# Projections with stationary weights: four high products, then four low ones

## The chip, the cores and the metric

The kernel runs on one core of one Trainium2 chip. The metric is the device time of one execution in microseconds (us); for the kernel before it is the median of three runs, 1385.38 us.

## The reference

One layer of a hybrid block on a sequence of 256 tokens with 2048 features, all in fp32. The input is normalised and multiplied with one wide matrix; its columns feed 16 attention heads of 128 (three dilated windows over the same keys), a chunked state-space scan (64 heads of 64, 8 groups, state 128) behind a short convolution, and several gates. Cut to what matters here:

```python
hn = rms_norm(x, norm_w)
proj = hn @ w_in                       # (256, 2048) @ (2048, 22592)
q, k, v, z_a, z_s, xbc, dt_raw, g_a, g_s = jnp.split(proj, split_points, axis=-1)
# attention: three (window, dilation) patterns over q, k, v, joined by their log-sum-exp
o_a = o_a.reshape(b, s, ATTN_WIDTH) * jax.nn.silu(z_a)
xbc = jax.nn.silu(causal_depthwise_conv(xbc, conv_w, conv_b))
xs, bm, cm = jnp.split(xbc, ...)
y = ssd_chunked_scan(xs, dt, a, bm, cm) + d_skip * xs
y = rms_norm(y * jax.nn.silu(z_s), ssm_norm_w)
merged = jax.nn.sigmoid(g_a) * (o_a @ w_attn_branch) + jax.nn.sigmoid(g_s) * (y @ w_ssm_branch)
return rms_norm(x + merged @ w_out, final_norm_w)
```

## The kernel before

**Split products.** Each fp32 operand of a large product is cut into a high part in the faster fp32r type and a low part, the rest. A product of two such operands is the sum of high x high, high x low and low x high. The input stands transposed in `XT`: for each of 16 blocks of 128 features (`KT`, index `kt`) 512 columns, 256 tokens of the high part followed by 256 tokens of the low part.

**Weights.** They come in units of 128 x 1024 in the order of a plan. `unit` (lines 269 to 281) waits for one unit `w`, has ScalarE write its high part `h` (L276) and VectorE its low part `l` (L277), and lets later work hang on that unit. Five buffers hold loaded units, four each hold `h` and `l`; a scheduler that orders instructions by priority and a modelled time line lays the streams of all engines, and units are split ahead at raised priority.

**Two ways to use them.** For wide outputs (`gemm_b`, `gemm_pair`: the gates, the value projection, the output matrices) a block of the input is the stationary operand and the weights stream through as 512 columns. For outputs that are needed transposed (B, C, xs, zs, q, k, za) `gemm_a` does the reverse: 128 x 128 weights are stationary and the input streams. A projection is 2 units of 8 blocks, and for each block two products go to one accumulator of 512 columns:

- high, L329: `h` is loaded as the stationary operand, all 512 columns of `XT` stream (high x high in the left half, high x low in the right),
- low, L332: `l` is loaded, the left 256 columns of `XT` stream, and their products are added to the right half.

`evac` adds both halves. There are 124 such projections: B and C for seven groups, 31 xs and 31 zs, 16 each of q, k and za.

**Other places named below.** `gemm_first` (L377 high, L378 low) computes four projections at once at the start, four accumulators for each block of the input; `gemm_dt` (L354) puts high and low weights into one stationary block; `gates` calls `gemm_b` (L412 to L414). Small jobs of the scan and of attention (transposes, scores, masks) are queued with a due time; `tick` and `run_due` in `gemm_a` release them at a projection's start and behind its first product.

Of the kernel before, what the change touches and what calls it, by code (L numbers as in the profile page):

```python
# [16 lines left out]
S = 256  # L17
# [6 lines left out]
KT = D // P  # L24
UNIT = 1024
UK = 8
UB = 2
SCALE = float(P) ** -0.5
L_AHEAD = 120
M_AHEAD = 200  # L30
# [166 lines left out]
def hybrid_block(ctx: ExitStack, tc: tile.TileContext, wall, xt, x, pk_d, cst_d, fw_d, out):  # L197
    nc = tc.nc
    ve, ac, gp, pe = nc.vector, nc.scalar, nc.gpsimd, nc.tensor
# [24 lines left out]
    def bank(tag, bufs, name):  # L224
        return ps.tile([P, 512], F32, name=name, tag=tag, bufs=bufs)
# [41 lines left out]
    def unit(n, shape):  # L267
        if n not in loaded:
            load(n)
        w = loaded.pop(n)  # L270
        h = stream.tile([P, UNIT], F32R, name=f"h{n}", tag="h", bufs=H_BUFS)
        l = stream.tile([P, UNIT], F32R, name=f"l{n}", tag="l", bufs=H_BUFS)
        cuts = (0, UNIT // 2, UNIT) if n < N_FINE else (0, UNIT)
        with tc.high_priority(L_AHEAD) if n >= KT // UB else nullcontext():
            for a, b in zip(cuts, cuts[1:]):
                ac.activation(h[:, a:b], w[:, a:b], AF.Copy)  # L276
                ve.tensor_tensor(l[:, a:b], w[:, a:b], h[:, a:b].bitcast(F32), ALU.subtract)  # L277
        for f in on_unit.pop(n, ()):
            f(h[:, 0:1].bitcast(F32))
        k, m = shape  # L280
        return h.rearrange("p (k m) -> p k m", k=k), l.rearrange("p (k m) -> p k m", k=k)
# [18 lines left out]
    now = [0]  # L300
# [6 lines left out]
    def run_due(until):  # L307
        while True:
            ready = [d for d in due if d[0] <= until]
            if not ready:  # L310
                break
            d = min(ready, key=lambda e: e[0])
            due.remove(d)
            d[1]()

    def tick(final=False):
        now[0] += 1
        run_due(float("inf") if final else now[0])

    def gemm_a(tag, xs_of, acc=None):  # L320
        tick()
        name = f"{tag[0]}{tag[1]}"
        acc = bank(acc, 2, f"ps_{name}") if acc else bank("g", 4, f"ps_{name}")
        for u in range(KT // UK):
            h, l = unit(FIRST[tag] + u, (UK, P))
            for kk in range(UK):
                kt = u * UK + kk
                m = xs_of(kt)
                pe.matmul(acc, h[:, kk, :], m, start=(kt == 0), stop=False)  # L329
                if kt == 0:  # L330
                    run_due(now[0] + 0.5)
                pe.matmul(acc[:, S:], l[:, kk, :], m[:, :S], start=False, stop=(kt == KT - 1))  # L332
        return acc

    def gemm_dt(src):
# [23 lines left out]
    def project(tag, acc=None):  # L359
        return gemm_a(tag, lambda kt: XT[:, kt, :], acc)  # L360

    def gemm_first(tag, prepare, load_on):
        name = f"{tag[0]}{tag[1]}"
        accs = [bank("g", 4, f"ps_{name}_{j}") for j in range(4)]
        for u in range(KT // UB):
            if u % 2 == 0:
                tick()
            for kk in range(UB):
                prepare(u * UB + kk)
            h, l = unit(FIRST[tag] + u, (UB, 512))  # L370
            load_on(u)
            for kk in range(UB):
                kt = u * UB + kk
# [273 lines left out]
    def load_on(u):  # L647
        if u:
            load(u + 4)
        if u < 3:  # L650
            nc.sync.dma_start(xr[:, 2 * u + 10 : 2 * u + 12, :], xt[:, 2 * u + 10 : 2 * u + 12, :])
        if u == 3:
            nc.sync.dma_start(pk[:, KT:], pk_d[:, KT:])
# [31 lines left out]
    with tc.tile_pool(name="ssm", bufs=2) as sp:  # L685
# [223 lines left out]
        for g in range(GROUPS):  # L909
# [9 lines left out]
            for t in range(max(4 * g, 1), 4 * g + 4):  # L919
                u, i = divmod(t, 2)  # L920
                acc = project(("xs", t))
# [19 lines left out]
                acc = project(("zs", t))  # L941
# [91 lines left out]
    with tc.tile_pool(name="att", bufs=2) as ap:  # L1033
# [4 lines left out]
        def scores(h, q, k, p):  # L1038
# [4 lines left out]
            slope = 2.0 ** (-8.0 * (h + 1) / NH)  # L1043
            ve.scalar_tensor_tensor(t, dist_c, slope / SCALE, sps[:, :384], ALU.mult, ALU.add)
            st = ap.tile([P, 8], F32, name=f"st{h}", tag="st", bufs=1)
            parts = ((0, P), (P, 384))
            for i, (a, b) in enumerate(parts):
                ve.tensor_reduce(st[:, i : i + 1], t[:, a:b], mybir.AxisListType.X, ALU.max)
            ve.tensor_scalar(st[:, 2:4], st[:, 0:2], -SCALE, None, ALU.mult)
            for i, (a, b) in enumerate(parts):  # L1050
                ac.activation(p[:, a:b], t[:, a:b], AF.Exp, scale=SCALE, bias=st[:, 2 + i : 3 + i])
            for i, (a, b) in enumerate(parts):
# [219 lines left out]
```

## Time and profile before

| | before |
|---|---|
| three runs | 1384.97, 1385.54, 1385.38 us |
| median | 1385.38 us |
| span of the profiled execution, first to last instruction | 1383.8 us |
| mean granted TensorE clock | 0.998 |
| products on TensorE (PE) | 7266 |
| splits into high and low parts, L276 and L277 | 398 instructions each |
| HBM traffic | 314.87 MB read, 28.77 MB written |

The profiled execution's own time outside its span was not recorded; the median stands 1.6 us above the span. In the profile, PE is TensorE's products and PEld its loads of stationary operands, which overlap them; DVE is VectorE, ACT ScalarE, POOL GpSimd, SP the queue that issues most transfers. A row of the timeline gives the start in us, the duration in us, the engine, the source line, the operation, the tile written and the tiles read, the shapes, and how many equal instructions were merged into the row. Since products are pipelined, the duration of one reaches past the start of the next.

### The profile page before, as it was taken

How to read it: one execution, taken by the hardware profiler on the slowest of the kernel's cores; microseconds unless marked ns; L12 is line 12 of the kernel's file. 1: busy time of each engine (PE TensorE's matmuls, PEld its weight loads, DVE VectorE, ACT ScalarE, POOL GpSimd, SP SyncE). 2: the span in 40 equal slices, each digit the busy share in tenths (PEclk: the TensorE clock that was granted, in tenths of full speed). 3: DMA queues.
4: the chain of work that ended last, by engine and by line, in shares of the span. 5: the costliest groups of instructions: out<-in, count | busy, mean ns of one | idle time of the engine just before them, and what ended most of it. 6: DMA issues, size and time to landing. Idle time of an engine off the chain costs nothing.

```text
span 1383.8 us, 20696 instructions
## 1 busy us (share of the span) xinstructions
PE 1373.6 (99%) x7266; PEld 1169.9 (85%) x7266; DVE 1169.5 (85%) x1753; ACT 835.5 (60%) x1306; POOL 142.0 (10%) x226
## 2 busy tenths in 40 slices
PE   9999999999999999999999999999999999999997
PEld 8888888888888888888888888888888888888886
DVE  7898999987799898789889897777877788888897
ACT  7656677675667675766565554544544556655564
POOL 2301111101011100010001001111111000000112
PEclk9999999999999999999999999999999999999999
DMA  9767988868787866668677668888888757865773
GB/s 347 231 187 225 313 254 291 279 224 287 245 266 240 294 212 208 188 224 280 230 259 267 222 209 278 275 275 273 299 288 301 241 161 264 294 222 180 243 273 122
DMA packets 105080, 345.00 MB, mean 249 GB/s; under 512 B 11728, under 2 KB 13712, under 8 KB 104976
## 3 DMA queue, kind: packets, MB, share of 16 engines
q1 hardware_dynamic: 103536, 339.62, 74.0%
q10 hardware_dynamic: 1440, 4.06, 0.8%
q8 instruction: 57, 0.93, 0.3%
q14 instruction: 47, 0.39, 0.1%
HBM read 314.87 MB, written 28.77 MB: 248 GB/s over the span
## 4 chain that ended last, share of the span: by engine, by line
PE 97%; DMA 1%; DVE 1%; ACT 1%; issue 0%; SPq 0%; POOL 0%; POOLq 0%; DVEq 0%; ACTq 0%
PE ps_zs L329 8%; PE ps_xs L329 8%; PE ps_zs L332 4%; PE ps_q L329 4%; PE ps_za L329 4%; PE ps_k L329 4%; PE ps_xs L332 4%; PE ps_ssm L476 3%; PE ps_ssm L477 3%; PE ps_ssm L478 3%; PE ps_q L332 2%; PE ps_k L332 2%; PE ps_za L332 2%; PE ps_gs L414 2%; PE ps_gs L412 2%; PE ps_gs L413 2%
## 5 line engine op out<-in xcount | busy, mean ns | idle before, releaser
L276 ACT ACTIVATE h<-w 128x1024 fp32r<-128x1024 f32 (+1 forms) x398 | 413.9, 1047 | 318.0 <-issue 78.8
L277 DVE TENSOR_TENSOR l<-w,h 128x1024 fp32r<-128x1024 f32 (+1 forms) x398 | 479.4, 1211 | 124.2 <-ACT h L276 121.8
L329 PE MATMUL ps_zs<-XT,h 128*128 128x512 f32 x496 | 176.3, 397 | 0.0
L329 PE MATMUL ps_xs<-XT,h 128*128 128x512 f32 x496 | 175.9, 396 | 0.0
L332 PE MATMUL ps_zs<-XT,l 128*128 128x256 f32 x496 | 139.9, 282 | 0.0
L332 PE MATMUL ps_xs<-XT,l 128*128 128x256 f32 x496 | 139.8, 282 | 0.0
L329 PEld LDWEIGHTS ps_xs<-XT,h 128*128 128x128 f32 x496 | 93.3, 188 | 21.7
L329 PEld LDWEIGHTS ps_zs<-XT,h 128*128 128x128 f32 x496 | 93.4, 188 | 21.2
L332 PEld LDWEIGHTS ps_zs<-XT,l 128*128 128x128 f32 x496 | 93.7, 189 | 1.5 <-issue 0.7
L332 PEld LDWEIGHTS ps_xs<-XT,l 128*128 128x128 f32 x496 | 93.7, 189 | 0.4
L329 PE MATMUL ps_q<-XT,h 128*128 128x512 f32 x256 | 92.5, 405 | 0.2 <-ACT h L276 0.2
L329 PE MATMUL ps_k<-XT,h 128*128 128x512 f32 x256 | 89.9, 395 | 0.0
L329 PE MATMUL ps_za<-XT,h 128*128 128x512 f32 x256 | 89.7, 394 | 0.0
L543 ACT ACTIVATE ha<-wa 128x1024 fp32r<-128x1024 f32 x43 | 45.4, 1055 | 46.4 <-DMA wa<-in_wall 10.9
L332 PE MATMUL ps_q<-XT,l 128*128 128x256 f32 x256 | 71.2, 278 | 0.0
L332 PE MATMUL ps_k<-XT,l 128*128 128x256 f32 x256 | 71.1, 278 | 0.0
L332 PE MATMUL ps_za<-XT,l 128*128 128x256 f32 x256 | 71.1, 278 | 0.0
L544 DVE TENSOR_TENSOR la<-wa,ha 128x1024 fp32r<-128x1024 f32 x43 | 52.5, 1220 | 11.9 <-ACT ha L543 11.8
L782 ACT ACTIVATE gt<-acb,acT 128x128 f32<-128x128 f32 x128 | 44.2, 391 | 23.7 <-DMA acb<-acum_d 21.9
L329 PEld LDWEIGHTS ps_q<-XT,h 128*128 128x128 f32 x256 | 48.2, 188 | 11.5 <-ACT h L276 0.6
L329 PEld LDWEIGHTS ps_za<-XT,h 128*128 128x128 f32 x256 | 48.1, 188 | 11.3
L329 PEld LDWEIGHTS ps_k<-XT,h 128*128 128x128 f32 x256 | 48.1, 188 | 11.2
(688 smaller groups left out, 3325.1 us busy)
## 6 DMA issues: line engine op xcount, KB each, us to landing
w<-in_wall SPq DMA_DIRECT2D x394, 512.0 KB, 4.7
wa<-in_wall SPq DMA_DIRECT2D x43, 512.0 KB, 4.9
th_a<-in_wall SPq DMA_DIRECT2D x19, 512.0 KB, 5.6
sums_at<-in_wall SPq DMA_DIRECT2D x18, 512.0 KB, 4.7
acb<-acum_d SPq DMA_DIRECT2D x32, 256.0 KB, 4.0
t_ssm<-sums_at SPq DMA_DIRECT2D x13, 512.0 KB, 4.1
wt<-t_ssm SPq DMA_DIRECT2D x13, 512.0 KB, 5.4
th_a<-in_wall SPq DMA_DIRECT2D x19, 256.0 KB, 6.0
```

The lines of the kernel that those rows point to most:

```text
L276: ac.activation(h[:, a:b], w[:, a:b], AF.Copy)
L277: ve.tensor_tensor(l[:, a:b], w[:, a:b], h[:, a:b].bitcast(F32), ALU.subtract)
L329: pe.matmul(acc, h[:, kk, :], m, start=(kt == 0), stop=False)
L332: pe.matmul(acc[:, S:], l[:, kk, :], m[:, :S], start=False, stop=(kt == KT - 1))
L412: pe.matmul(accs[i], xh, h[:, kk], start=(kt == 0), stop=False)
L413: pe.matmul(accs[i], xh, l[:, kk], start=False, stop=False)
L476: pe.matmul(acc, xh, h, start=start, stop=False)
L477: pe.matmul(acc, xh, l, start=False, stop=False)
L478: pe.matmul(acc, xl, h, start=False, stop=stop)
L543: ac.activation(h, src, AF.Copy)
L544: ve.tensor_tensor(l, src, h.bitcast(F32), ALU.subtract)
L782: ac.activation(g4[:, n, b], acb[:, j, b // 2 * P : b // 2 * P + P], AF.Relu, scale=-1.0, bias=sc[:, h : h + 1],)
```

## The change

In `gemm_a` the eight blocks of a unit are taken in two runs of four (`A_RUN = 4`). Within a run the four high products come first and the four low ones after them. Before, each high product was followed by the low product of its block. The operands, shapes, accumulators and the flags that start and end an accumulation are those of before; the due jobs are still released behind the first product of a projection.

```diff
+A_RUN = 4
...
         for u in range(KT // UK):
             h, l = unit(FIRST[tag] + u, (UK, P))
-            for kk in range(UK):
-                kt = u * UK + kk
-                m = xs_of(kt)
-                pe.matmul(acc, h[:, kk, :], m, start=(kt == 0), stop=False)
-                if kt == 0:
-                    run_due(now[0] + 0.5)
-                pe.matmul(acc[:, S:], l[:, kk, :], m[:, :S], start=False, stop=(kt == KT - 1))
+            for k0 in range(0, UK, A_RUN):
+                for kk in range(k0, k0 + A_RUN):
+                    kt = u * UK + kk
+                    pe.matmul(acc, h[:, kk, :], xs_of(kt), start=(kt == 0), stop=False)
+                    if kt == 0:
+                        run_due(now[0] + 0.5)
+                for kk in range(k0, k0 + A_RUN):
+                    kt = u * UK + kk
+                    pe.matmul(acc[:, S:], l[:, kk, :], xs_of(kt)[:, :S], start=False, stop=(kt == KT - 1))
```

The lines below it move by three, `gemm_a`'s own to L330 (high) and L335 (low). What becomes of it on PE, first at the end of a projection of xs (the tiles `h` and `l` are the parts of one unit, numbers tell buffers apart), where the next one, zs, begins. Before:

```order
L332 MATMUL ps_xs_4292<-XT,l_4296 128x256
L329 MATMUL ps_xs_4292<-XT,h_4295 128x512
L332 MATMUL ps_xs_4292<-XT,l_4296 128x256
L329 MATMUL ps_xs_4292<-XT,h_4317 128x512
L329 MATMUL ps_zs_4356<-XT,h_4359 128x512
L332 MATMUL ps_xs_4292<-XT,l_4318 128x256
L329 MATMUL ps_xs_4292<-XT,h_4317 128x512
L332 MATMUL ps_xs_4292<-XT,l_4318 128x256
L329 MATMUL ps_xs_4292<-XT,h_4317 128x512
```

After:

```order
L330 MATMUL ps_xs_4292<-XT,h_4317 128x512 x4
L335 MATMUL ps_xs_4292<-XT,l_4318 128x256 x4
L330 MATMUL ps_xs_4292<-XT,h_4317 128x512 x4
L335 MATMUL ps_xs_4292<-XT,l_4318 128x256 x4
L330 MATMUL ps_zs_4356<-XT,h_4359 128x512 x4
L335 MATMUL ps_zs_4356<-XT,l_4360 128x256 x4
```

High and low products took turns before, but for one product of zs that the scheduler had drawn ahead, so that two high ones stood together; now they stand in fours, and here zs begins behind xs.

The second place is a projection of B with small jobs inside it (`dt_tp` transposes, `cbp` scores of the scan). Before:

```order
L329 MATMUL ps_B_1195<-XT,h_1198 128x512
L742 MATMUL dt_tp<-cst,early 128x64 x2
L768 MATMUL cbp_1024<-ct_401,bt_400 128x256
L769 MATMUL cbp_1024<-ct_401,bt_400 128x128
L742 MATMUL dt_tp<-cst,early 128x64 x2
L332 MATMUL ps_B_1195<-XT,l_1199 128x256
```

After:

```order
L335 MATMUL ps_B_1195<-XT,l_1199 128x256 x2
L745 MATMUL dt_tp<-cst,early 128x64 x2
L771 MATMUL cbp_1024<-ct_401,bt_400 128x256
L772 MATMUL cbp_1024<-ct_401,bt_400 128x128
L335 MATMUL ps_B_1195<-XT,l_1199 128x256 x2
L330 MATMUL ps_B_1195<-XT,h_1198 128x512 x4
L335 MATMUL ps_B_1195<-XT,l_1199 128x256 x2
L745 MATMUL dt_tp<-cst,early 128x64 x2
L335 MATMUL ps_B_1195<-XT,l_1199 128x256 x2
```

The jobs stood in one group between a high and a low product; now they stand in two groups, each inside a run of low ones.

## The prediction

> **What bounds the kernel now.** I read the busy table first, then the chain that ended last, then what TensorE waited for. On the page:
>
> ```profile
> PE 1373.6 (99%) x7266; PEld 1169.9 (85%) x7266; DVE 1169.5 (85%) x1753; ACT 835.5 (60%) x1306; POOL 142.0 (10%) x226
> PEclk9999999999999999999999999999999999999999
> PE 97%; DMA 1%; DVE 1%; ACT 1%; issue 0%; SPq 0%; POOL 0%; POOLq 0%; DVEq 0%; ACTq 0%
> ```
>
> In the table of waits on PE:
>
> ```profile
> PE warm L623 <- DVE ssq L620: 1.4, 1, 1.4
> PE ps_first L377 <- ACT h L276: 0.3, 1, 0.3
> PE ps_q L329 <- ACT h L276: 0.2, 1, 0.2
> ```
>
> TensorE is busy 99% of the span, is 97% of the last chain, has its full clock in every slice, and waits for other engines 1.9 us in all, 1.4 us of them before the first product. So the time is the number of products times the spacing at which TensorE starts them. A product's listed duration overlaps the next product, so spacings have to be read from starts. How many products the change touches, by stage (line 329 alone; the x behind PE busy is the count):
>
> ```profile
> 74.00:558.00 484.00, 427.01 (x1216) 228.28 (x1216) 1.00 0.78 252
> 828.00:1120.00 292.00, 270.13 (x767) 144.21 (x767) 1.00 0.82 273
> ```
>
> By the code there are 124 projections of 16 pairs: 1984 pairs, each one high product (512 columns, L329) and one low (256 columns, L332). The two windows hold 1983 of the high ones.
>
> **What one pair costs now.** The timeline of PE in two stretches where only these pairs run. From 533.20 to 549.10 there are 45 of each, from 317.92 to 346.00 there are 81 (first and last row of each):
>
> ```profile
> 533.20 0.40 PE L329 MATMUL ps_xs<-XT,h 128*128 128x512 f32 x1
> ...
> 549.10 0.40 PE L329 MATMUL ps_xs<-XT,h 128*128 128x512 f32 x1
> ```
>
> ```profile
> 317.92 0.39 PE L329 MATMUL ps_B<-XT,h 128*128 128x512 f32 x1
> ...
> 346.00 0.39 PE L329 MATMUL ps_zs<-XT,h 128*128 128x512 f32 x1
> ```
>
> 15.90 us / 45 = 353.3 ns, and 28.08 us / 81 = 346.7 ns. The same instructions in the same order run at two spacings, each held for tens of us. All the steps from one high product to the next over one low one, from the first to the last below, are 1908 in the timeline and average 349.4 ns: about four tenths of them long.
>
> ```profile
> 76.79 0.39 PE L329 MATMUL ps_xs<-XT,h 128*128 128x512 f32 x1
> ...
> 1119.20 0.39 PE L329 MATMUL ps_za<-XT,h 128*128 128x512 f32 x1
> ```
>
> What turns the short spacing into the long one can be seen where one projection overlaps the next and two high products stand together:
>
> ```profile
> 387.40 0.39 PE L329 MATMUL ps_C<-XT,h 128*128 128x512 f32 x1
> ...
> 390.87 0.39 PE L329 MATMUL ps_xs<-XT,h 128*128 128x512 f32 x1
> 391.10 0.39 PE L329 MATMUL ps_zs<-XT,h 128*128 128x512 f32 x1
> ...
> 391.44 0.40 PE L329 MATMUL ps_xs<-XT,h 128*128 128x512 f32 x1
> ...
> 392.85 0.40 PE L329 MATMUL ps_xs<-XT,h 128*128 128x512 f32 x1
> ```
>
> Ten pairs up to 390.87 take 3.47 us (347 ns each); after the double the four pairs from 391.44 take 1.41 us (352 ns each). So the strict turn high, low, high, low can hold the short spacing, and breaking the turn can lose it.
>
> **The change, part by part.** It removes nothing and adds nothing: the same 1984 + 1984 products, loads of stationary weights, transfers, splits and evictions. It moves three low products of every four behind the high ones. On PE 475 runs of exactly four high and 488 of four low come out, so it does what it says; the few other products (transposes, scores, scan) stand in 58 groups where there were 57. No wait is added. A low half is first needed three high products later than before, a high half of a unit is read out one run of low ones earlier; with the waits above near zero neither gain is worth anything, and the cover is that both halves are ready ahead now. If it were gone, the price is what such a wait costs, 0.2 to 0.3 us each by those rows. On SP, POOL, ACT and DVE some neighbours swap places; no transfer waits show on PE, so I take zero.
>
> What is left is the spacing in runs of four. The kernel has a place that already does this: the first projection (L377 high, L378 low, four accumulators) starts its units in runs of four and four, its later ones partly in turn. PE timeline there:
>
> ```profile
> 10.87 1.08 PE L377 MATMUL ps_first<-yTa,h 128*128 128x512 f32 x4
> 12.25 1.09 PE L377 MATMUL ps_first<-yTa,h 128*128 128x512 f32 x4
> 13.18 0.63 PE L378 MATMUL ps_first<-yTa,l 128*128 128x256 f32 x4
> 13.65 1.09 PE L377 MATMUL ps_first<-yTa,h 128*128 128x512 f32 x4
> ...
> 19.27 0.40 PE L377 MATMUL ps_first<-yTb,h 128*128 128x512 f32 x1
> ...
> 20.66 1.09 PE L377 MATMUL ps_first<-yTb,h 128*128 128x512 f32 x4
> ...
> 22.06 0.40 PE L377 MATMUL ps_first<-yTb,h 128*128 128x512 f32 x1
> ...
> 23.47 1.11 PE L377 MATMUL ps_first<-yTb,h 128*128 128x512 f32 x4
> ...
> 24.89 0.40 PE L377 MATMUL ps_first<-yTb,h 128*128 128x512 f32 x1
> ...
> 26.28 1.08 PE L377 MATMUL ps_first<-yTb,h 128*128 128x512 f32 x4
> ...
> 27.67 0.40 PE L377 MATMUL ps_first<-yTb,h 128*128 128x512 f32 x1
> ```
>
> Nine blocks of four and four: 10.87 to 12.25 (1.38 us), five in a row from 12.25 to 19.27 (7.02), then 1.40, 1.42 and 1.39. Together 12.61 us / 36 pairs = 350.3 ns; the five in a row alone 351.0; the cheapest 345 to 347, the dearest 355. Within a block (12.25, 13.18, 13.65) the high four take 0.93 us (232 ns each) and the low four 0.47 us (117.5 ns each). So runs neither reach the short spacing for good nor fall to something new.
>
> A run of products of one shape alone, for comparison: the gate stage (L412 to L414, all 512 columns, 40 products between the first two rows), and the dt projection, 16 high-width products in a row that start out of step:
>
> ```profile
> 60.93 0.39 PE L414 MATMUL ps_gs<-h,yTa 128*128 128x512 f32 x1
> ...
> 69.99 0.39 PE L412 MATMUL ps_gs<-h,yTb 128*128 128x512 f32 x1
> ```
>
> ```profile
> 29.08 2.03 PE L354 MATMUL ps_dt<-yTa,h 128*128 128x512 f32 x8
> 30.94 1.98 PE L354 MATMUL ps_dt<-yTb,l 128*128 128x512 f32 x8
> 32.77 0.39 PE L412 MATMUL ps_gs<-h,yTa 128*128 128x512 f32 x1
> ```
>
> 9.06 / 40 = 226.5 ns steady; in the dt projection the first eight take 232.5 ns each and the next eight 229: settling takes more than eight products, a run of four is too short for it. A short pair (346.7) is 226.5 plus 120 for the low product.
>
> The sum: (350.3 - 349.4) ns x 1984 = +1.8 us. Bounds from the rows: all pairs at the short spacing, -2.7 x 1984 = -5.4 us; all at the long one, +3.9 x 1984 = +7.7 us; all as the dearest block, +5.6 x 1984 = +11 us. I take the mean of the nine blocks, the nearest rows there are. The profiled span is 1383.8 us, the median 1385.4 us, so 1.6 us lie around it; span 1385.6 us, time **1387.2 us**.
>
> A rule that speaks against any effect: the Trainium skill, SBUF — State Buffer, section Who interferes with whom, gives TensorE two independent read ports, one for the moving operand and one for weight loads. By it the place of the loads would not change the spacing, and the sum would be 0. The two spacings above, for one and the same order, are not explained by that rule, but no row shows that the loads cause them.
>
> **The rivals.**
>
> *The short spacing holds in runs* (25%). For it: the blocks from 10.87 and from 26.28 took 345 and 347 ns per pair, and in the attention stage the turn holds the short spacing almost throughout, so a good start after each head could last. Against: in the first projection it was lost again within one block. Price -2 to -5.4 us, 1380.0 to 1383.4 us.
>
> *Runs hold the long spacing: the slower side* (23%). Each change from four high to four low breaks the turn as the double at 391.10 did, and four products are too few to settle. It decides from 350.8 ns per pair on (1.4 ns x 1984 = 2.8 us). At 351.0, the five blocks in a row, 1388.6 us; at 353.3, 1393.1 us. Against: the mean over nine blocks lies below.
>
> *Low runs get cheaper than any row* (6%). Were a low run to cost half of a steady 512-column product, 113 ns, the pair would be 226.5 + 113 = 339.8 ns, -9.6 x 1984 = -19 us, 1366 us. Against it: the low four at 117.5 ns above. The skill has such a rule: TensorE: Matmul & The Clock Gate, section Back-to-back issue gap, gives columns / 2.4 + 2.5 ns for an isolated spacing, 216 and 109 ns; a pair of 325 would be an estimate of -48 us. The steady 226.5 ns disagrees with it, and the measurement decides.
>
> *The weight load shows* (1%). A load lasts 189 ns:
>
> ```profile
> L332 PEld LDWEIGHTS ps_zs<-XT,l 128*128 128x128 f32 x496 | 93.7, 189 | 1.5 <-issue 0.7
> ```
>
> If loads could not overlap, a low run would go at 189 ns and the pair at 416: +130 us. The four low at 117.5 ns exclude it, since loads then overlap.
>
> **How the numbers follow.** The forecast itself, a mixture of both spacings between 349 and 350.8 ns, -1 to +2.8 us, has 45%. A measurement of this kernel tells 0.2% (2.8 us) from no change. Faster by more: most of the short-spacing rival and the cheap low runs, 22 + 6 = 28%. Slower by more: the long-spacing rival, the load and a little of the forecast's upper end, 28%. Within: 44%. Range 1380 to 1392 us: from all pairs short to most pairs long; outside lie the cheap low runs and the dearest blocks. The forecast's own range is 1384.4 to 1388.2 us.
>
> **What would show it.** In the new profile, starts from one run of four high to the next, divided by four: near 350 ns with blocks of both kinds proves the step; 346.7 throughout the attention stage proves the first rival; 351 to 353 throughout the second; low runs at 113 the third. Waits on PE beyond 3 us, or more groups of other products among the runs, would make the step that takes the rest as zero wrong.

## The result and the profile after

| | before | after |
|---|---|---|
| median of 20 runs each on one chip | 1385.51 us (1384.77 to 1386.75) | 1388.12 us (1387.19 to 1389.09) |
| ratio after / before, 95% interval | | 1.0019 (1.0013 to 1.0025) |
| span of the profiled execution | 1383.8 us | 1386.5 us |
| mean granted TensorE clock | 0.998 | 0.999 |

The change costs 2.6 us, at the edge of the 0.2% that were called no change. The forecast was 1387.2 us.

From the page of the changed kernel, the busy table and the chain that ended last by engine:

```profile
PE 1376.0 (99%) x7266; PEld 1172.5 (85%) x7266; DVE 1170.0 (84%) x1753; ACT 837.6 (60%) x1306; POOL 145.9 (11%) x226
PE 97%; DMA 1%; DVE 1%; ACT 1%; issue 0%; SPq 0%; POOL 0%; POOLq 0%; DVEq 0%; ACTq 0%
```

The table of waits on PE has two rows left:

```profile
PE warm L626 <- DVE ssq L623: 1.4, 1, 1.4
PE ps_first L380 <- ACT h L277: 0.6, 1, 0.6
```

The same number of products, the same bound, 2.0 us of waits where there were 1.9. The 2.4 us that PE is busy for longer are spacing. The stages show where. These are the first products of the value projection, of the gate stage behind attention, and of the attention branch's output in the timeline of before (the first product of xs, 76.79, stands in the prediction):

```profile
748.54 0.39 PE L476 MATMUL ps_v<-h,XT 128*128 128x512 f32 x1
...
1121.34 0.58 PE L476 MATMUL ps_ga<-h,XT 128*128 128x512 f32 x1
...
1204.92 0.39 PE L476 MATMUL ps_attn<-h,oaTa 128*128 128x512 f32 x1
```

The same places in the timeline of the changed kernel, with the first product of xs:

```profile
77.42 1.07 PE L330 MATMUL ps_xs<-XT,h 128*128 128x512 f32 x4
...
749.06 0.39 PE L479 MATMUL ps_v<-h,XT 128*128 128x512 f32 x1
...
1124.07 0.58 PE L479 MATMUL ps_ga<-h,XT 128*128 128x512 f32 x1
...
1207.64 0.39 PE L479 MATMUL ps_attn<-h,oaTa 128*128 128x512 f32 x1
```

| stretch | before, us | after, us | difference |
|---|---|---|---|
| start to first xs | 76.79 | 77.42 | +0.6 |
| first xs to first v: scan stage with B, C, xs, zs, then the scan's output matrix | 671.75 | 671.64 | -0.1 |
| first v to first ga: attention stage with q, k, za | 372.80 | 375.01 | +2.2 |
| first ga to first attn: the gate stage | 83.58 | 83.57 | 0.0 |

The scan stage has 76 of the 124 changed projections and lost nothing; the attention stage has 48 and lost 2.2 us. Of the 0.6 us ahead of xs, 0.3 are the longer wait of `ps_first`; they are not stable: in the runs below that stretch takes 76.3 to 77.4 us.

In what follows, the turn is the order of before (high, low, high, low), a pair is one high and one low product, and a block is a run of four high products with its four low ones. How runs of four are spaced in the changed kernel, first in the scan stage (timeline of PE; x4 is four products in one row):

```profile
540.17 1.09 PE L330 MATMUL ps_zs<-XT,h 128*128 128x512 f32 x4
541.10 0.64 PE L335 MATMUL ps_zs<-XT,l 128*128 128x256 f32 x4
541.58 1.09 PE L330 MATMUL ps_zs<-XT,h 128*128 128x512 f32 x4
...
547.19 1.09 PE L330 MATMUL ps_xs<-XT,h 128*128 128x512 f32 x4
```

and in the attention stage, from the jobs ahead of a projection of q on:

```profile
1013.02 0.60 PE L1044 MATMUL sps<-kT,qT 128*128 128x256 f32 x2
1013.27 1.28 PE L330 MATMUL ps_q<-XT,h 128*128 128x512 f32 x4
1014.39 0.63 PE L335 MATMUL ps_q<-XT,l 128*128 128x256 f32 x4
1014.86 1.08 PE L330 MATMUL ps_q<-XT,h 128*128 128x512 f32 x4
...
1016.25 1.09 PE L330 MATMUL ps_q<-XT,h 128*128 128x512 f32 x4
...
1021.87 1.09 PE L330 MATMUL ps_k<-XT,h 128*128 128x512 f32 x4
```

540.17 to 547.19 is 7.02 us for five blocks of four pairs, 351.0 ns per pair. The first block behind the jobs starts almost together with the last of them; the second goes at some 348 ns (1014.86 to 1016.25, 1.39 us / 4; 348.75 by the nanoseconds of the trace), and from the next block on it is 351 again (1016.25 to 1021.87, 5.62 us / 16). From the third undisturbed block on, nearly all blocks of the trace, in both stages, repeat in a cycle of two, 350.25 and 351.5 ns per pair, whatever stands ahead of them: 350.85 on average. With the cheaper first ones counted in, undisturbed blocks average 350.5 ns in the scan stage (266 of them) and 350.7 ns in the attention stage (159). Inside such a cycle the starts of the single products lie 233, 236, 228, 232 (high), 118, 119, 118, 116 (low), 235, 234, 235, 225, 117, 120, 120, 120 ns apart.

The turn of before, in the attention stage (29 pairs between these rows of its timeline):

```profile
999.81 0.39 PE L329 MATMUL ps_k<-XT,h 128*128 128x512 f32 x1
...
1009.86 0.40 PE L329 MATMUL ps_za<-XT,h 128*128 128x512 f32 x1
```

10.05 us / 29 = 346.6 ns. Taken by stage, the steps of before that the prediction averaged over at 349.4 ns are 350.6 ns in the scan stage (1173 of them) and 347.5 ns in the attention stage (735). Against 350.85 that gives +0.25 ns x 76 x 16 = +0.3 us for the scan stage and +3.35 ns x 48 x 16 = +2.6 us for attention; with the means over all undisturbed blocks it is -0.1 and +2.5 us. The table has -0.1 and +2.2.

### The profile page after: what moved, and what is told of

Read it like the earlier page. It is cut to its first block, busy times and chain, and to the rows that moved or that the text cites. A ratio compares the mean times of both kernels' runs of the same rounds, so it can differ in the third digit from the quotient of the medians.

```text
span 1386.5 us, 20710 instructions
## 1 busy us (share of the span) xinstructions
PE 1376.0 (99%) x7266; PEld 1172.5 (85%) x7266; DVE 1170.0 (84%) x1753; ACT 837.6 (60%) x1306; POOL 145.9 (11%) x226
## 4 chain that ended last, share of the span: by engine, by line
PE 97%; DMA 1%; DVE 1%; ACT 1%; issue 0%; SPq 0%; POOL 0%; POOLq 0%; DVEq 0%; ACTq 0%
PE ps_zs L330 8%; PE ps_xs L330 8%; PE ps_q L330 4%; PE ps_za L330 4%; PE ps_k L330 4%; PE ps_zs L335 4%; PE ps_xs L335 4%; PE ps_ssm L479 3%; PE ps_ssm L480 3%; PE ps_ssm L481 3%; PE ps_k L335 2%; PE ps_za L335 2%; PE ps_q L335 2%; PE ps_gs L417 2%; PE ps_gs L415 2%; PE ps_gs L416 2%
## 5 line engine op out<-in xcount | busy, mean ns | idle before, releaser
L330 PE MATMUL ps_zs<-XT,h 128*128 128x512 f32 x496 | 137.1, 396 | 0.0
L330 PE MATMUL ps_xs<-XT,h 128*128 128x512 f32 x496 | 137.0, 395 | 0.0
L330 PEld LDWEIGHTS ps_zs<-XT,h 128*128 128x128 f32 x496 | 84.9, 189 | 12.4 <-issue 1.2
L330 PEld LDWEIGHTS ps_xs<-XT,h 128*128 128x128 f32 x496 | 84.8, 189 | 11.0
L335 PEld LDWEIGHTS ps_xs<-XT,l 128*128 128x128 f32 x496 | 76.1, 189 | 10.5
L335 PEld LDWEIGHTS ps_zs<-XT,l 128*128 128x128 f32 x496 | 75.9, 189 | 10.3
L335 PE MATMUL ps_zs<-XT,l 128*128 128x256 f32 x496 | 78.9, 281 | 0.0
L335 PE MATMUL ps_xs<-XT,l 128*128 128x256 f32 x496 | 78.9, 281 | 0.0
L330 PE MATMUL ps_q<-XT,h 128*128 128x512 f32 x256 | 72.5, 405 | 0.1
L330 PE MATMUL ps_k<-XT,h 128*128 128x512 f32 x256 | 70.1, 395 | 0.0
L330 PE MATMUL ps_za<-XT,h 128*128 128x512 f32 x256 | 69.9, 394 | 0.0
L547 DVE TENSOR_TENSOR ltu<-wa,htu 128x1024 fp32r<-128x1024 f32 x38 | 46.3, 1219 | 11.2 <-ACT htu L546 11.2
L546 ACT ACTIVATE htu<-wa 128x1024 fp32r<-128x1024 f32 x38 | 40.0, 1054 | 21.2 <-PE ps_ssm L481 7.0
L330 PEld LDWEIGHTS ps_q<-XT,h 128*128 128x128 f32 x256 | 44.8, 189 | 7.1 <-ACT h L277 0.6
L330 PEld LDWEIGHTS ps_k<-XT,h 128*128 128x128 f32 x256 | 43.8, 189 | 5.9
L764 DVE SCALAR_TENSOR_TENSOR cv_x<-raw_x,cw,cv_x 128x256 f32<-128x256 f32 x93 | 44.6, 480 | 5.0 <-ACT cv_x L762 4.0
L330 PEld LDWEIGHTS ps_za<-XT,h 128*128 128x128 f32 x256 | 43.7, 189 | 5.9
```

What stands on the lines that cost most here:

```text
L330: pe.matmul(acc, h[:, kk, :], xs_of(kt), start=(kt == 0), stop=False)
L335: pe.matmul(acc[:, S:], l[:, kk, :], xs_of(kt)[:, :S], start=False, stop=(kt == KT - 1))
L546: ac.activation(h, src, AF.Copy)
L547: ve.tensor_tensor(l, src, h.bitcast(F32), ALU.subtract)
L764: ve.scalar_tensor_tensor(h, raw[:, 1 + k : 1 + k + S], cw[:, 48 * k + ct : 48 * k + ct + 1], h, ALU.mult, ALU.add)
```

## The experiments

The theory after the result, A: each order of the products has a spacing of its own that it keeps everywhere (runs of four 350.85 ns); the turn alone has two, and what ran ahead decides which. A change of order then costs, in each stage, its own spacing less the one that the stage had. The letters in the quoted expectations are the theories that each run set against each other. All ratios are against the kernel before on the same chip, with 95% intervals.

**1 and 2. Half of the change at a time.** Runs of four in the attention stage alone, then in the scan stage alone:

```diff
+        A_RUN = 4 if tag[0] in ("q", "k", "za") else 1     # e1_attn4
+        A_RUN = 1 if tag[0] in ("q", "k", "za") else 4     # e2_scan4
```

> Runs of four in q, k and za alone; B, C, xs and zs keep the turn. Theory A (runs settle at one spacing of 350.9 ns per pair; what they cost depends on the spacing that the turn held there, 347.5 ns in the attention stage and 350.6 in the scan's stage): nearly all of the loss is here, 3.4 ns x 768 pairs = +2.6 us against before. Rival B (runs cost every pair the same 1.4 ns): 768 pairs are +1.1 us.

> Runs of four in B, C, xs and zs alone; q, k and za keep the turn. Theory A: 0.2 ns x 1216 pairs = +0.3 us, within half a us of before. Rival B: 1216 pairs are +1.7 us.

Attention alone: 1388.35 us against 1385.66, ratio 1.0019 (1.0011 to 1.0028), +2.7 us. Scan stage alone: 1385.75 us, ratio 1.0000 (0.9991 to 1.0009), +0.1 us. The high products of q, first to last start, in the view by tile of before:

```profile
L329 PE MATMUL ps_q<-XT,h x256: 390/395/580, 824.9 to 1108.4; 128*128 128x512 f32 x128
```

of the changed kernel:

```profile
L330 PE MATMUL ps_q<-XT,h x256: 387/396/580, 825.3 to 1110.7; 128*128 128x512 f32 x128
```

of the first experiment:

```profile
L330 PE MATMUL ps_q<-XT,h x256: 387/396/580, 824.7 to 1110.1; 128*128 128x512 f32 x128
```

and of the second:

```profile
L330 PE MATMUL ps_q<-XT,h x256: 389/395/579, 824.8 to 1108.4; 128*128 128x512 f32 x128
```

The distance is 283.5, 285.4, 285.4 and 283.6 us. The durations of a product (395 or 396 ns, the median in the middle) say nothing; only the starts do. The whole loss is the attention stage's, as A had it (+2.6 and +0.3). B, a loss spread over all pairs (+1.1 and +1.7), is out.

**3. What sets the turn's spacing: due jobs behind the low product.** The turn is kept, and the small jobs no longer stand between a high product and its low one:

```diff
                 pe.matmul(acc, h[:, kk, :], m, start=(kt == 0), stop=False)
+                pe.matmul(acc[:, S:], l[:, kk, :], m[:, :S], start=False, stop=(kt == KT - 1))
                 if kt == 0:
                     run_due(now[0] + 0.5)
-                pe.matmul(acc[:, S:], l[:, kk, :], m[:, :S], start=False, stop=(kt == KT - 1))
```

> The turn of before, but the small jobs due in a projection are released behind its first low product and not between its first high and low. Theory C (which spacing the turn holds is set by what follows a break: jobs followed by a high product leave the short spacing, jobs followed by a low product, or two high ones together, leave the long one): the scan's jobs stop starting the long spacing; the pairs of that stage fall from 350.6 to 348 or less, -2 to -4 us in all, the attention stage stays. Rival D (it is chance which spacing follows): within 1 us of before, both spacings as often.

1387.39 us, ratio 1.0012 (1.0003 to 1.0021), +1.7 us: the opposite sign of C. D's band of 1 us is left by the median, but the interval (+0.4 to +2.9 us) reaches into it. First xs to first v took 673.25 us (before 671.75), and the stage's mean pair is 351.7 instead of 350.6 ns. By the starts, all six groups of score jobs of the scan (`cbp`) that now stand behind a low product are followed by the long spacing, which five of them met already; between a high and its low product they had left the spacing as it was in five of seven places and begun the long one in two. All four groups of transposes of xs and nearly all jobs of attention (14 of 15 groups of scores) that are followed by a high product leave the short one. So that the turn is broken does not decide by itself. Why one job leaves the one spacing and another the other stays open.

**4. The same with the order pinned.** Both products of the pair are kept in program order as well, so that no high product is drawn ahead:

```diff
+                in_order(pe.matmul(acc, h[:, kk, :], m, ...))
+                in_order(pe.matmul(acc[:, S:], l[:, kk, :], m[:, :S], ...))
```

> As the run before, and every product of a projection is kept in program order, so that no product of the next projection is drawn ahead and no two high ones stand together. Theory C: nothing is left that starts the long spacing; 346.7 ns per pair in nearly all of the 1984 pairs, -4 to -5.4 us. Rival D: within 1 us of before.

1402.46 us, ratio 1.0118 (1.0103 to 1.0134), +16.8 us. This run tells more of pinning than of the spacing. Its two longest waits on PE:

```profile
PE dt_tp L742 <- DVE early L727: 9.7, 1, 9.7
PE xtp L801 <- DVE xs L397: 2.5, 1, 2.5
```

and its busy time in stretches (PE, PEld, DVE, ACT, POOL, then the granted clock, the DMA share and GB/s):

```profile
80.00:95.00 15.00, 7.99 (x46) 6.68 (x44) 13.97 (x32) 6.90 (x12) 0.23 (x2) 0.84 0.61 189
95.00:105.00 10.00, 6.71 (x25) 5.50 (x26) 4.55 (x14) 1.22 (x5) 0.00 (x0) 0.55 0.10 33
```

Program order put the time steps' transposes ahead of projections that were ready, PE stood 9.7 us for them, and afterwards the granted clock was 0.55 for a stretch of 10 us. The second wait, 2.5 us up to 133.42, was followed by the same: five pairs from 134.75 to 137.95 us are 640 ns apart, at a granted clock of 0.50. The scan stage's undisturbed pairs are at 351.0 ns on average, some six tenths of them long, so C's short spacing throughout did not come here either; with so much else changed this weighs less than the third run.

**5 and 6. Other run lengths.** Two, and eight:

```diff
-A_RUN = 4
+A_RUN = 2     # e5_run2
+A_RUN = 8     # e6_run8
```

> Runs of two high and two low in all projections. Theory A (an order of widths settles at spacings of its own, whatever came before it; four and four has one, 350.9 ns per pair): one or two values that repeat from block to block, somewhere between 346.7 and 353.4 ns. Rival E (each change between the two widths costs, long runs save it): more than 351 ns per pair, +3 us or more against before.

> Runs of eight high and eight low. Theory A: a value of its own between 346.7 and 353.4 ns. Rival E: half as many changes as in runs of four, so half of their excess over 346.7 ns: 348.8 ns per pair, -1.2 us against before, 4 us below the runs of four.

Runs of two: 1384.01 us, ratio 0.9989 (0.9980 to 0.9999), 1.6 us below before. Timeline of PE, in the scan stage and in the attention stage:

```profile
536.29 0.63 PE L330 MATMUL ps_zs<-XT,h 128*128 128x512 f32 x2
536.76 0.40 PE L335 MATMUL ps_zs<-XT,l 128*128 128x256 f32 x2
...
540.48 0.63 PE L330 MATMUL ps_zs<-XT,h 128*128 128x512 f32 x2
...
1000.09 0.63 PE L330 MATMUL ps_k<-XT,h 128*128 128x512 f32 x2
...
1002.88 0.63 PE L330 MATMUL ps_za<-XT,h 128*128 128x512 f32 x2
```

4.19 us / 12 pairs = 349 and 2.79 us / 8 = 349; over longer stretches 348.4 ns in both stages. The first xs to first v got 1.9 us shorter, v to ga 0.8 longer: again near the spacing of the order less that of the stage. E, by which the pair gets dearer the more often the width changes, said over 351 ns and is out: twice as many changes as in runs of four are cheaper.

Runs of eight: 1387.14 us, ratio 1.0012 (1.0003 to 1.0021), +1.5 us.

```profile
401.67 2.00 PE L330 MATMUL ps_xs<-XT,h 128*128 128x512 f32 x8
403.51 1.11 PE L335 MATMUL ps_xs<-XT,l 128*128 128x256 f32 x8
404.46 2.00 PE L330 MATMUL ps_zs<-XT,h 128*128 128x512 f32 x8
```

The eight high take 1.84 us (230 ns each), the eight low 0.95 us (119), 2.79 us / 8 = 349 ns. The single steps show how a run settles: high 233, 236, 229, 232, 231, then 227, 227, 227 ns; low 113, 119, then 120. So after a change of width five high products are dear (+28 ns in all), the first low one is cheap (-7 ns), and then the stream goes at 226.7 and 120. By the stages, xs to v got 1.8 us shorter and v to ga 1.1 longer, but ga to attn 1.4 longer, with two new waits on PE:

```profile
PE pp_ga L480 <- DVE ltu L547: 0.5, 1, 0.5
PE pp_ga L479 <- ACT htu L546: 0.3, 1, 0.3
```

The longer run seems to move work of the other engines at the edge of the next stage, and there it is late; this run alone does not show it.

**7. Do the weight loads bear on the spacing?** The turn, with low products that load only 64 of 128 stationary columns (all but a projection's last one). This leaves out the low part of the weights for outputs 64 to 127.

```diff
+                n = P if kt == KT - 1 else 64
-                pe.matmul(acc[:, S:], l[:, kk, :], m[:, :S], start=False, stop=(kt == KT - 1))
+                pe.matmul(acc[:n, S:], l[:, kk, :n], m[:, :S], start=False, stop=(kt == KT - 1))
```

> The turn of before, but of all low products save the last of a projection only 64 of the 128 stationary columns are loaded and multiplied; the other half of the low part's outputs is left out. Same order, same streamed columns. Theory F (a load of the next stationary block takes slots from the product that streams meanwhile, about 13 ns of 227): the high products, under which the low blocks are loaded, get about 7 ns shorter, -10 to -14 us, and the loads of L332 shorter than 189 ns. Rival G (the 13 ns are a fixed cost of a product, and the two spacings a matter of widths alone): within 2 us of before.

1379.68 us, ratio 0.9956 (0.9943 to 0.9970), -6.0 us. The groups by line, shapes apart (mean ns of one behind the busy time):

```profile
L333 PEld LDWEIGHTS ps_zs<-XT,l 128*64 128x64 f32 x465 | 63.8, 137 | 1.5 <-issue 0.9 <-DVE sums_at L453 0.2 <-DVE xs L398 0.2
L329 PE MATMUL ps_zs<-XT,h 128*128 128x512 f32 x496 | 174.3, 393 | 0.0
```

The low load takes 137 ns instead of 189. The listed duration of a high product stays (393 ns), yet the mean pair is 346.2 ns where it was 349.4. Two spacings show again, 340 ns (steps of 227 and 113 ns, as in the four pairs from 114.93 to 116.29) and, in most places, 346.6 ns (229 and 117.5 to 118); those of the turn are 346.7 ns (230 and 117) and 353.3 ns (236 and 117.5). If the lower one answers to the lower, each lies 6.7 ns below that of the turn; the gain is then 6 and not the 10 to 14 us that F expected because the upper one holds for longer here: 340 ns stand in 9% of the steps in the scan stage and 30% in attention. G (no effect) is out. The edit halves the columns that the low product itself multiplies as well as its load, so the run does not isolate the load. What speaks for it is within the run: the one full low product of each projection starts 233 ns behind its high product, the half ones from the second to the fifteenth 229 ns on average; up to its start the full one differs by its load alone. So a load seems to cost something although it overlaps. The Trainium skill, SBUF — State Buffer, section Who interferes with whom, counts separate read ports for the moving operand and for loads; the prediction took from it that the place of the loads leaves the spacing alone, and the 3.2 ns that the mean pair lost speak against that conclusion. Whether the place is a port, the array or the order of issue is not shown.

**8. Holding the short spacing in the scan stage.** xs and zs from the thirteenth on are kept in program order, where no wait is near:

```diff
+                keep = in_order if tag[0] in ("xs", "zs") and tag[1] >= 12 else (lambda i: i)
+                keep(pe.matmul(acc, h[:, kk, :], m, ...))     # the low product likewise
```

> The turn of before, with the products of xs and zs from the thirteenth on kept in program order, so that the eight places where two high products stand together are gone. Theory H (such a pair of high products starts the long spacing, which then lasts until the group's next transposes): some 126 us of long spacing become short, 1.9% of them, -2.4 us. Rival D (chance, or the jobs alone set it): within 0.7 us of before.

1384.07 us, ratio 0.9987 (0.9979 to 0.9996), -1.6 us; first xs to first v 670.18 us (-1.6), the stage's mean pair 349.3 instead of 350.6 ns. H's direction, at two thirds of its size: without two high products side by side (a double, as at 391.10 in the prediction) the short spacing lasts to the next scan or score jobs, and in seven places these still begin the long one. So a double is one cause among several.

**9. Sixteen: all high products of a projection, then all low ones.**

```diff
+        run = 16
+        units = []
+        for k0 in range(0, KT, run):
+            while len(units) * UK < k0 + run:
+                units.append(unit(FIRST[tag] + len(units), (UK, P)))
+            for kt in range(k0, k0 + run):
+                pe.matmul(acc, <high of kt>, xs_of(kt), ...)
+            for kt in range(k0, k0 + run):
+                pe.matmul(acc[:, S:], <low of kt>, xs_of(kt)[:, :S], ...)
```

> All sixteen high products of a projection, then its sixteen low ones, in all projections; both units of a projection are split before its first low product. Theory J (a step from 256 to 512 columns costs some 28 ns until the high products have settled at 227 ns, after about five of them; a step from 512 to 256 gains 7; runs shorter than that stay unsettled): 227 and 120 ns for the settled products, 346.7 + 20 / 16 = 347.9 ns per pair, -1.5 ns x 1984 = -3.0 us against before. Rival K (runs of eight were already at their floor of 349.2): -0.4 us. Where the low parts are held too long for the four buffers, waits on PE for ACT or DVE take part of it back.

1385.94 us, ratio 1.0002 (0.9993 to 1.0011), +0.25 us. Where nothing stands inside a projection or ahead of it, the pair is what J worked out from the settling, 347.9 ns in both stages, and first xs to first v is 2.7 us shorter. But from ga to attn it takes 87.41 us, 3.8 more. Timeline of PE there:

```profile
1134.49 0.39 PE L480 MATMUL ps_ga<-hc,sx_x 128*128 128x512 f32 x1
1136.36 0.50 PE L478 MATMUL pp_ga<-htu,sx_x 128*128 128x512 f32 x1 [1.48 <-ACT htu L545]
...
1138.17 0.63 PE L479 MATMUL pp_ga<-ltu,sx_x 128*128 128x512 f32 x1
1138.59 0.63 PE L480 MATMUL pp_ga<-htu,sx_x 128*128 128x512 f32 x1
...
1141.15 0.53 PE L478 MATMUL ps_ga<-h,XT 128*128 128x512 f32 x1
```

and the stretches ahead of the slow steps and with them, columns as above:

```profile
1134.00:1137.00 3.00, 1.52 (x6) 0.68 (x5) 0.66 (x1) 1.75 (x2) 0.00 (x0) 1.00 0.48 194
1137.00:1142.00 5.00, 4.78 (x15) 3.71 (x15) 4.77 (x5) 3.82 (x5) 0.00 (x0) 0.66 0.56 178
```

PE waits 1.48 us for a split (ACT L545) and 0.22 us for another, and from 1138.17 on a product starts every 0.42 to 0.43 us: seven steps to 1141.15 take 2.98 us, 426 ns each, where a product alone in its stretch steps at 226.5. The granted clock is 0.66 from 1137 to 1142. The Trainium skill, TensorE: Matmul & The Clock Gate, section HAM oscillation — how this bites in real kernels, asks for idle gaps above some 3.4 us before the clock halves; here 1.87 us between two starts, 1.48 us of them idle, were followed by it, so the measurement decides. The gain was given back by a wait and the clock behind it. That a run over both units of a projection makes the splits at the stage's edge late is argued here; the eleventh run bears it out.

**10 and 11. A different order for each stage.** Runs of two, then of sixteen, in the scan stage and the first two heads; the turn for all later heads, where it holds the short spacing:

```diff
-        run = 16
+        run = 1 if tag[0] in ("q", "k", "za") and tag[1] > 1 else 2      # e10_two_then_turn
+        run = 1 if tag[0] in ("q", "k", "za") and tag[1] > 1 else 16     # e11_sixteen_then_turn
```

> Runs of two in B, C, xs, zs and the first two heads, where the turn held the long spacing for most of the time; the turn from the third head on, where it holds the short one. Theory A (each order keeps its own spacing in its own place): the scan's stage as with runs of two everywhere, -1.9 us, the first two heads -0.4 us, the later heads as before: -2.3 us against before, 0.7 us below runs of two everywhere. Rival D (the later heads' short spacing depends on what ran ahead of them): no gain over runs of two everywhere.

> As the run before, with runs of sixteen in place of runs of two. Theory J: 347.9 ns in place of 350.6 in the scan's stage, -3.3 us, and -0.4 us in the first two heads: -3.7 us against before. Rival K: -1.9 us.

Two then turn: 1382.78 us, ratio 0.9980 (0.9971 to 0.9989), -2.9 us. Sixteen then turn: **1382.54 us, ratio 0.9976 (0.9967 to 0.9986), -3.15 us**, faster than both kernels. Its timeline of PE in the scan stage:

```profile
397.62 3.82 PE L330 MATMUL ps_xs<-XT,h 128*128 128x512 f32 x16
401.27 2.08 PE L334 MATMUL ps_xs<-XT,l 128*128 128x256 f32 x16
403.18 3.82 PE L330 MATMUL ps_zs<-XT,h 128*128 128x512 f32 x16
```

5.56 us / 16 = 347.5 ns: the high ones 3.65 us / 16 = 228, the low ones 1.91 us / 16 = 119.5. First xs to first v is 669.02 us (-2.7), v to ga 372.05 (-0.75), ga to attn 83.58 as before: with the turn at the stage's edge the late split and its wait are gone. Of the expectations, A had -2.3 for the tenth run; its 372.57 us from v to ga, where runs of two took 373.64, speak against D, by which the later heads gain nothing. J had -3.7 for the eleventh, inside the interval (-4.6 to -1.9 us), with K at its edge; the 347.9 ns per pair speak for J.

**12. Equal widths.** The turn, with low products that stream all 512 columns; this adds low x low to the right half:

```diff
-                pe.matmul(acc[:, S:], l[:, kk, :], m[:, :S], start=False, stop=(kt == KT - 1))
+                pe.matmul(acc, l[:, kk, :], m, start=False, stop=(kt == KT - 1))
```

> The turn of before, but a low product streams all 512 columns (it adds low x low, which before leaves out), so that all products of a projection have one width. Theory J (it is the change of width that unsettles): no long spacing is left, 226.7 ns for every product, 453.4 ns per pair, +104 ns x 1984 = +206 us. Rival M (stationary weights as such go at 231 to 235 ns): 464 to 470 ns per pair, +227 to +240 us.

1592.65 us, ratio 1.1493 (1.1472 to 1.1514), +207.0 us (J: +206; M: 227 or more). Timeline of PE, six products between these rows:

```profile
399.89 0.39 PE L329 MATMUL ps_zs<-XT,h 128*128 128x512 f32 x1
...
401.25 0.39 PE L329 MATMUL ps_zs<-XT,h 128*128 128x512 f32 x1
```

1.36 us / 6 = 226.7 ns. No second spacing holds anywhere, although a full load stands ahead of each product; steps of 231 to 236 ns stand only in the first nine products behind other work. So stationary weights as such do not cost the time. The run changes a second thing, though. A load begins at about the start of the product ahead of its own. In the turn of before, a load of `h` with the product that uses it:

```profile
320.58 0.19 PEld L329 LDWEIGHTS ps_B<-XT,h 128*128 128x128 f32 x1
320.69 0.39 PE L329 MATMUL ps_B<-XT,h 128*128 128x512 f32 x1
```

and in this run:

```profile
400.12 0.19 PEld L329 LDWEIGHTS ps_zs<-XT,h 128*128 128x128 f32 x1
400.35 0.39 PE L329 MATMUL ps_zs<-XT,h 128*128 128x512 f32 x1
```

Behind a product of 256 columns a load of 0.19 us has 0.11 us until its own product starts, behind one of 512 columns 0.23. Equal widths take away the change of width and the short lead of the load at once, so which of the two unsettles the stream is open.

## Why the prediction was right, and one term too small

- **The bound: right.** TensorE's spacing sets the time; waits, loads that show, transfers and neighbours that swap places came to next to nothing (2.0 us of waits in all, 0.3 us more at `ps_first`). The second experiment, with 76 projections rearranged and +0.1 us, shows it best.
- **Runs neither keep the short spacing nor fall to something new: right.** The short-spacing rival is refuted by the attention stage: behind the jobs one block goes at some 348 ns, the next at 351. Cheap low runs at 113 ns and loads that show are refuted by the 117 to 120 ns of the low steps.
- **The size of the pair: the term that was too small.** The sum took 350.3 ns, the mean of nine blocks in the first projection. Measured are 350.85 in settled blocks. Of those nine, only the five in a row (351.0) stood as the change makes most of them stand, block behind block; the first stood ahead of that row, three stood between stretches of the turn, and these four go at 345 to 355 ns, 349.4 on average. With 350.85 the sum is +1.45 ns x 1984 = +2.9 us, with all undisturbed blocks counted (350.5 and 350.7) about +2.3; measured are +2.6 in the medians, and in the profiled runs +2.1 in the two stages and +0.6 at the start, where nothing was changed. That blocks of so different kinds averaged to within 0.3 ns of the mean that came is luck. The long-spacing rival's lower end, 1388.6 us at 351.0, was the better reading of the same rows, though not its upper end: 353.3 belongs to the turn alone.
- **Why runs of four do not settle: right, with a wrong count.** The dt projection was read as needing more than eight products. Behind a run of low ones it takes five (runs of eight and sixteen), so four are just too few. The short pair is not the settled 226.5 + 120 ns either, as the prediction had it, but 230 + 117.
- **Where the loss is: not in the sum.** It was made with one mean over both stages, 349.4 ns. By stages it would have said that the scan stage (350.6) loses next to nothing and that attention (347.5) pays nearly all of it, as the first two experiments show. The prediction noted that attention holds the short spacing, and used it for a rival only.
- **Both kinds of blocks: half right.** A mixture of blocks at 347 and 353 ns was expected; what came is one cycle, 350.25 and 351.5, with a cheap block only behind a disturbance.
- **What breaks the turn: half right.** Doubles of high products began the long spacing in four of the six places of before where the short one stood ahead of them, and keeping the order gained 1.6 us; but scan and score jobs do so as well, and moving jobs behind the low product did not help (+1.7 us).

Shown: the spacings of the orders, that those of runs hold in both stages, that the attention stage pays for the change, and that the stream is unsettled behind a change from 256 to 512 columns and steady with equal widths. Argued: that the load takes part in it. Open: whether the change of width or the load's short lead unsettles the stream, and why a given job leaves the turn in the one or the other spacing.

## What to carry to other kernels

When TensorE is the bound, read spacings from starts and by stage, and price a new order as its own repeating spacing less the one that each stage has now; take the repeating spacing from blocks that stand behind each other, not from single ones. The best order can differ from stage to stage: here sixteen and sixteen where the turn was disturbed, the turn where it held, and each alone was worse. An order that is longer or pinned has to be looked at where the next stage begins, since a wait of 1.5 us there cost 3.8 us.

## What the runs showed of the hardware

- Settled streams of products with a full load each step at 226.7 ns (512 columns) and 120 ns (256 columns). Behind a change from 256 to 512 columns it takes five products and 28 ns to settle (runs of eight and sixteen); the change back gives 7 ns.
- Per pair of one high and one low product: turn 346.7 or 353.3 ns; runs of two 348.4; four 350.85; eight 349.2; sixteen 347.9. The dependence on the run's length is not monotonic: four is the dearest of the four lengths of runs.
- With half a load of the low product (137 instead of 189 ns) and half its columns, the mean pair of the turn fell from 349.4 to 346.2 ns, although loads are hidden behind products. With equal widths and full loads there is one spacing only.
- A load, listed at 0.19 us, starts 0.11 us ahead of its product when that stands behind one of 256 columns, and 0.22 to 0.24 us ahead behind one of 512.
- A wait of 1.48 us on TensorE (1.87 us between two starts) was followed by about 3 us at 426 ns per product, granted clock 0.66 in the window of 5 us (ninth run; the slices of its page do not show it). A wait of 2.5 us was followed by 3.2 us at 640 ns per pair and a granted clock of 0.50 (fourth run).
